# A two-layer transformer trunk on one core: the attention rounds put into traced order, in two groups of matmul steps instead of four

## The chip, the cores and the metric

One core of a Trainium2 chip runs the whole program. Its engines are TensorE (PE, with its weight loads shown as PEld), VectorE (DVE), ScalarE (ACT), GpSimd (POOL) and SyncE (SP, which issues the weight transfers). The metric is the device time of one execution in microseconds (us); a kernel is timed several times and the median is compared.

## The reference

Two decoder layers over 256 tokens of width 1024. Each layer is a half-step SwiGLU (width 2816), an attention mixer, a second half-step SwiGLU and a gated layer input. The mixer of the first layer is latent attention (called MLA below), that of the second is forgetting attention (FOX); both have 16 heads and are causal. Cut to the mixers:

```python
def mla_mixer(hn, pos, w_in, g_q_lat, w_uq, g_kv_lat, w_ukv, g_qn, g_kn, w_o):
    z = hn @ w_in                                   # c_q 512, c_kv 256, k_pe 32
    q = rms_norm(c_q, g_q_lat) @ w_uq               # 16 heads x 96
    kv = rms_norm(c_kv, g_kv_lat) @ w_ukv           # 16 heads x (64 of k, 64 of v)
    k = concatenate([k_nope, k_pe of every head])
    q, k = rms_norm per head, rope on the last 32
    return attention(q, k, v) @ w_o
def fox_mixer(hn, w_in, b_f, g_qn, g_kn, w_o):
    q, k, v, f = split(hn @ w_in)                   # 16 heads x 64 each, 16 gates
    return attention(rms_norm(q), rms_norm(k), v, cumsum(log_sigmoid(f + b_f))) @ w_o
def attention(q, k, v, decay=None):                 # blocks of 128 queries
    probs = softmax(mask(q @ k.T * scale + decay[t] - decay[s]))
    return probs @ v
```

## The kernel before, in words

**Dense products.** A weight unit of up to 1 MB is loaded by SP into one of three `raw` buffers. ScalarE rounds it to `whi` (L92) and VectorE writes the rest to `wlo` (L94), in pieces of up to 1024 columns; six pieces of each can be alive. Activations are kept as two such halves too. A dense product is then three fp32r matmuls on TensorE (`mm_w` L212 to L214, `mm_x` L225 to L227) or two in the feed-forward part (`mm_wide` L219, L220). I call these the dense matmuls.

**Attention.** The heads are worked in eight pairs per layer (class `Pair`). A pair passes four steps on TensorE: `turn` transposes its queries and keys (L543 in `heads_t`, four transposes each), and ScalarE copies the queries' transposes (`qt`, L547) and VectorE the keys' (`kt`, L545) out of PSUM; `weigh` multiplies them (L449, L450), after which VectorE masks and takes the maximum (L454), ScalarE takes the exponentials (L465), VectorE divides (L470); `turn_back` transposes the weights (L478) and a copy per head goes to `pt` (L481 on ScalarE, L483 on VectorE); `mix` multiplies them with the values (L490, L495; the two heads go to columns 0 to 63 and 64 to 127 of the array), and the result is split into two halves again (L499 on ScalarE, L294 on VectorE). All these steps take their PSUM tiles from one pool `pb` of four buffers.

**Rounds.** `mixed` weaves the pairs with the dense matmuls that are still to do: first the two last head groups of keys and queries (`late`, run by `Rows.run(amount)`, where an amount of 1 is about 1 us of dense work), then the output projection (`OutProj`). A round takes `weigh` of one pair, `turn_back` of the pair before it, `turn` of the next pair, `mix` of the second pair before, with a quarter of the dense amount behind each. Before the rounds MLA computes its latents: `zmm(c, ...)` is the product of column group c, and `latent(c)` reads it out of PSUM in a chain of ScalarE and VectorE steps that ends in a square `zq` (L696, L697, L701). `keys(g)` and `queries(g)` are the head groups' products.

**What sets the order.** The program is traced in the order of the Python code, and a scheduler then orders each engine's instructions. An instruction that went through `steady(...)` or `order(...)` while that object is on is pinned behind the instruction traced before it on its engine. In the kernel before, `steady` is off in both mixers, so that the scheduler places the attention steps and the dense matmuls as its own estimate of readiness says. Every engine runs its instructions in the order in which they then stand. At the end `OutProj.rest` does the last rows of the output projection in four parts `dp`; behind each part VectorE adds it to the residual `h` (L294). Parts 0 and 1 lie in one PSUM tile, and so do parts 2 and 3, so that part 1 is written after the addition of part 0 has read the tile.

Of the kernel before, what the change touches and what calls it, by code (L numbers as in the profile page):

```python
# [16 lines left out]
P = 128  # L17
S = 256
D = 1024
KD = D // P  # L20
# [109 lines left out]
def trunk(ctx: ExitStack, tc: tile.TileContext, a: dict, out: bass.AP):  # L130
    nc = tc.nc
# [17 lines left out]
    order = Order(tc)  # L149
# [57 lines left out]
    steady = Order(tc)  # L207
# [24 lines left out]
    for dp in range(4):  # L232
        c = slice(dp * 256, (dp + 1) * 256)
# [24 lines left out]
    ident = const.tile([P, P], F32, name="ident")  # L258
# [174 lines left out]
    class Pair:  # L433
# [10 lines left out]
        def weigh(self):  # L444
            pool, dk, qt, kt, rq = self.pool, self.dk, self.qt, self.kt, self.rq
            self.sm = []
            for hd in range(2):
                sp = pb()
                nc.tensor.matmul(sp[:, :P], lhsT=qt[:dk, hd, :P], rhs=kt[:dk, hd, :P], start=True, stop=True)  # L449
                nc.tensor.matmul(sp[:, P : 3 * P], lhsT=qt[:dk, hd, P:], rhs=kt[:dk, hd, :], start=True, stop=True)  # L450
# [12 lines left out]
                for tt, (c0, c1) in enumerate(((0, P), (P, 3 * P))):  # L463
                    sc = 1.0 if rq is None else rq[:, tt, hd : hd + 1]
                    nc.scalar.activation(  # L465
                        sm[:, c0:c1], sm[:, c0:c1], AF.Exp, bias=mx[:, 2 + tt : 3 + tt], scale=sc, accum_out=mx[:, 4 + tt : 5 + tt]
                    )
                nc.vector.reciprocal(mx[:, 6:8], mx[:, 4:6])
                for tt, (c0, c1) in enumerate(((0, P), (P, 3 * P))):
                    nc.vector.tensor_scalar(sm[:, c0:c1], sm[:, c0:c1], mx[:, 6 + tt : 7 + tt], None, op0=ALU.mult)  # L470
                self.sm.append(sm)

        def turn_back(self):
            self.pt = []
            for hd in range(2):
                tp = pb()
                for c in range(3):
                    nc.tensor.transpose(tp[:, c * P : (c + 1) * P], self.sm[hd][:, c * P : (c + 1) * P], ident)  # L478
                pt = self.pool.tile([P, 3 * P], F32, name="pt", tag="pt", bufs=4)
                if hd:  # L480
                    nc.scalar.copy(pt, tp[:, : 3 * P])  # L481
                else:
                    nc.vector.tensor_copy(pt, tp[:, : 3 * P])  # L483
                self.pt.append(pt)

        def mix(self):
            v, j, o = self.v, self.j, self.o
            op = pb()
            for n in range(2):
                nc.tensor.matmul(  # L490
                    op[n * 64 : n * 64 + 64, :S], lhsT=v[:, 0, 2 * j + n, :], rhs=self.pt[n][:, :S],
                    start=True, stop=False, skip_group_check=True,
                )
            for n in range(2):
                nc.tensor.matmul(  # L495
                    op[n * 64 : n * 64 + 64, P:S], lhsT=v[:, 1, 2 * j + n, :], rhs=self.pt[n][:, S:],
                    start=False, stop=True, skip_group_check=True,
                )
            nc.scalar.copy(o[:, j, 0, :], op[:, :S])  # L499
            tt_op(o[:, j, 1, :], op[:, :S], o[:, j, 0, :].bitcast(F32), ALU.subtract)  # L500
# [36 lines left out]
    def heads_t(pool, src, dk, name, scale):  # L537

        t = pool.tile([P, 2, S], F32, name=name, tag=name)
        tp = pb().rearrange("p (h t) -> p h t", h=2)  # L540
        for hd in range(2):
            for tt in range(2):
                nc.tensor.transpose(tp[:dk, hd, tt * P : (tt + 1) * P], src[:, tt, hd, :], ident)  # L543
        if scale is None:
            nc.vector.tensor_copy(t[:dk], tp[:dk])  # L545
        else:
            nc.scalar.activation(t[:dk], tp[:dk], AF.Copy, scale=scale)  # L547
        return t
# [90 lines left out]

    def mixed(early, late, each, ready, pair, o, after):  # L640

        order.on = True
        order.on = True
        Rows(*early).all()
        order.on = False
        order.on = False
        rows = Rows(*late)
        pairs = []
        for j in range(-1, KD + 2):
            if j == 5:  # L650
                rows.all()
            if 0 <= j - 1 < KD:
                pairs[j - 1].weigh()
                rows.run(each / 4)
            if j >= 2:
                pairs[j - 2].turn_back()
                rows.run(each / 4)
            if 0 <= j < KD:
                while not ready(j // 2):
                    rows.run(0.5)  # L660
                pairs.append(pair(j))
                pairs[j].turn()
                rows.run(each / 4)
            if j >= 2:
                pairs[j - 2].mix()
                if j == 5:
                    proj = OutProj(o, after)
                    rows = Rows(proj.first())
                    each = 3.6
                rows.run(each / 4)  # L670
        rows.all()
        proj.rest()


    def mla(norm, after, pool):
# [45 lines left out]
        sp = pb()  # L721
# [39 lines left out]
        got, ready = {}, set()  # L761
# [6 lines left out]
        v = pool.tile([P, 2, HEADS, VD], F32, name="v", tag="v", bufs=1)  # L768
        o = act.tile([P, KD, 2, S], F32R, name="xa", tag="xa")
# [92 lines left out]
        mixed([keys(0), queries(0), keys(1), queries(1)], [keys(2), queries(2), keys(3), queries(3)], 4, lambda g: g in ready, pair, o, after)  # L862


    def fox(norm, after, pool):
# [4 lines left out]
        got = {}  # L870
# [11 lines left out]
        v = pool.tile([P, 2, HEADS, VD], F32, name="v", tag="v", bufs=1)  # L882
# [87 lines left out]
        def more(g):  # L970
            yield from group(384)
            if g == 0:
                sums()
                decay(0)
            values(got.pop("ps"), 6 * g, 6)
# [6 lines left out]
        mixed([dense(0), more(0), dense(1)], [more(1), dense(2), dense(3)], 8, lambda g: len(got.get(g, ())) == 2, pair, o, after)  # L982


    def p_parts(i):
# [181 lines left out]
```

## Time and profile before

| | us |
|---|---|
| median of 3 runs | 1064.84 (1064.81 to 1066.46) |
| the profiled execution's own time | 1063.61 |
| its span, from first to last instruction | 1061.9 |
| PE busy | 1041.3 |
| DVE, ACT, POOL busy | 791.5, 591.9, 81.2 |

The profiled execution is 1.23 us below the median. A busy time counts an engine as busy while any of its instructions runs, so gaps between starts that are longer than usual do not all show as idle time; steps from start to start in the timeline show them. A row of the timeline merges instructions that are alike and follow each other; "x4" is their number. fp32 matmuls that are not transposes have two records each.

### The profile page before, as it was taken

Reading aid. Unit: us, or ns where it says so; the run is one execution under the profiler, and the core shown is the slowest. Engines: PE = TensorE matmul, PEld = TensorE weight load, DVE = VectorE, ACT = ScalarE, POOL = GpSimd, SP = SyncE. Lnnn points to the kernel's source line nnn. Section 1 sums busy time; section 2 is a strip of 40 time slices with the busy share of each in tenths; the row PEclk is TensorE's granted clock in tenths of the full one; section 3 lists DMA queues with packets and bytes.
Section 4 is the critical chain, followed back from the end, with each engine's and each line's share of the span. In section 5 each row is a group of like instructions: output and inputs, shape, how many; then the busy total and the mean of one; then the engine's idle time right before and its main releaser. Section 6 shows DMA issues by size and latency. Waiting matters only on the chain.

```text
span 1061.9 us, 16312 instructions
## 1 busy us (share of the span) xinstructions
PE 1041.3 (98%) x6368; PEld 918.9 (87%) x6368; DVE 791.5 (75%) x1364; ACT 591.9 (56%) x896; POOL 81.2 (8%) x107
## 2 busy tenths in 40 slices
PE   6999999999999999999999999999999999999998
PEld 4888888987898888888988888889999988888886
DVE  7979666679978877676987777558788797766665
ACT  4655544558766655554665555445566665554452
POOL 4000000133201000000110000011000100000010
PEclk9999999999999999999999999999999999999999
DMA  7755555534334755556447555654643266555541
GB/s 234 232 191 179 189 172 194 169 101 165 105 130 150 228 181 194 178 179 208 164 136 247 185 176 175 199 163 147 191 157 117 92 198 202 195 189 173 194 159 40
DMA packets 171089, 182.60 MB, mean 172 GB/s; under 512 B 6078, under 2 KB 164356, under 8 KB 171012
## 3 DMA queue, kind: packets, MB, share of 16 engines
q1 hardware_dynamic: 170164, 180.77, 52.1%
q8 instruction: 50, 0.82, 0.3%
q10 hardware_dynamic: 848, 0.79, 0.2%
q14 instruction: 27, 0.22, 0.1%
HBM read 180.50 MB, written 1.05 MB: 171 GB/s over the span
## 4 chain that ended last, share of the span: by engine, by line
PE 91%; DVE 4%; issue 1%; DMA 1%; POOL 1%; ACT 1%; ACTq 0%; DVEq 0%; POOLq 0%
PE pa L219 45%; PE pa L220 23%; PE pa L225 3%; PE pa L227 3%; PE pa L226 3%; PE pa L212 2%; PE pa L214 2%; PE pa L213 2%; DVE wlo L94 2%; PE pb L543 1%; PE pb L450 1%; PE pb L490 1%; PE pb L478 1%; DMA raw<-in_x_dram 1%; PE pb L449 1%
## 5 line engine op out<-in xcount | busy, mean ns | idle before, releaser
L94 DVE TENSOR_TENSOR wlo<-raw,whi 128x1024 fp32r<-128x1024 f32 (+3 forms) x357 | 425.4, 1204 | 203.6 <-ACT whi L92 203.0
L92 ACT CAST whi<-raw 128x1024 fp32r<-128x1024 f32 (+3 forms) x357 | 356.7, 1011 | 328.5 <-PE pa L219 192.9
L219 PE MATMUL pa<-xa,whi 128*128 128x512 f32 x1408 | 498.1, 397 | 1.7 <-DVE gt L294 0.9
L220 PE MATMUL pa<-xa,wlo 128*128 128x256 f32 x1408 | 396.6, 282 | 3.7 <-DVE wlo L94 3.7
L219 PEld LDWEIGHTS pa<-xa,whi 128*128 128x128 f32 x1408 | 265.4, 189 | 65.0 <-DVE gt L294 1.7
L220 PEld LDWEIGHTS pa<-xa,wlo 128*128 128x128 f32 x1408 | 264.6, 188 | 5.0 <-DVE wlo L94 4.9
L219 PE MATMUL pa<-hid,whi 128*128 128x512 f32 x704 | 244.2, 393 | 0.0
L220 PE MATMUL pa<-hid,wlo 128*128 128x256 f32 x704 | 195.0, 277 | 0.0
L219 PEld LDWEIGHTS pa<-hid,whi 128*128 128x128 f32 x704 | 132.0, 188 | 30.7
L220 PEld LDWEIGHTS pa<-hid,wlo 128*128 128x128 f32 x704 | 132.2, 188 | 0.0
L332 POOL TENSOR_TENSOR sq<-sq 128x512 f32<-128x512 f32 x24 | 35.6, 1481 | 833.6 <-ACT sq L330 805.0
L225 PE MATMUL pa<-whi,xa 128*128 128x256 f32 (+3 forms) x192 | 59.1, 308 | 0.0
L227 PE MATMUL pa<-whi,xa 128*128 128x256 f32 (+3 forms) x192 | 57.7, 301 | 0.0
L226 PE MATMUL pa<-wlo,xa 128*128 128x256 f32 (+3 forms) x192 | 57.4, 299 | 0.0
L212 PE MATMUL pa<-xa,whi 128*128 128x256 f32 x184 | 54.3, 295 | 0.0
L214 PE MATMUL pa<-xa,wlo 128*128 128x256 f32 x184 | 51.9, 283 | 0.0
L213 PE MATMUL pa<-xa,whi 128*128 128x256 f32 x184 | 51.9, 282 | 0.0
L321 DVE SCALAR_TENSOR_TENSOR xa<-h,gvec,xa 128x256 fp32r<-128x256 f32 x64 | 40.8, 679 | 2.6 <-ACT xa L319 2.6
L225 PEld LDWEIGHTS pa<-whi,xa 128*128 128x128 f32 x192 | 36.2, 189 | 1.4 <-issue 0.5
L319 ACT ACTIVATE xa<-h,gvec 128x256 fp32r<-128x256 f32 x64 | 29.0, 502 | 14.2 <-DVE h L294 12.4
L226 PEld LDWEIGHTS pa<-wlo,xa 128*128 128x128 f32 x192 | 36.2, 188 | 0.8
L227 PEld LDWEIGHTS pa<-whi,xa 128*128 128x128 f32 x192 | 36.0, 188 | 0.9
(262 smaller groups left out, 1184.0 us busy)
## 6 DMA issues: line engine op xcount, KB each, us to landing
raw<-in_ffn_w_in_dram SPq DMA_DIRECT2D x85, 1024.0 KB, 5.0
raw<-in_ffn_w_out_dram SPq DMA_DIRECT2D x32, 1024.0 KB, 5.2
raw<-in_ffn_w_out_dram SPq DMA_DIRECT2D x16, 768.0 KB, 4.8
raw<-in_ple_w_gate_dram SPq DMA_DIRECT2D x8, 1024.0 KB, 5.1
raw<-in_fox_w_in_dram SPq DMA_DIRECT2D x8, 1024.0 KB, 6.1
raw<-in_mla_w_o_dram SPq DMA_DIRECT2D x4, 1024.0 KB, 4.9
raw<-in_fox_w_o_dram SPq DMA_DIRECT2D x4, 1024.0 KB
raw<-in_mla_w_in_dram SPq DMA_DIRECT2D x3, 1024.0 KB, 5.9
```

The costliest lines, as they stand in the source:

```text
L92: self.order(self.nc.scalar.copy(h[:, part, :], whole))
L94: self.nc.vector.tensor_tensor(low[:, part, :], whole, h[:, part, :].bitcast(F32), op=ALU.subtract)
L212: steady(nc.tensor.matmul(ps, lhsT=hi, rhs=x[:, k, 0, :], start=start, stop=False, skip_group_check=True))
L213: steady(nc.tensor.matmul(ps, lhsT=hi, rhs=x[:, k, 1, :], start=False, stop=False, skip_group_check=True))
L214: return steady(nc.tensor.matmul(ps, lhsT=lo, rhs=x[:, k, 0, :], start=False, stop=stop, skip_group_check=True))
L219: steady(nc.tensor.matmul(ps, lhsT=hi, rhs=x[:, k], start=start, stop=False, skip_group_check=True))
L220: return steady(nc.tensor.matmul(ps[:, 1, :], lhsT=lo, rhs=x[:, k, 0, :], start=False, stop=stop, skip_group_check=True))
L225: steady(nc.tensor.matmul(ps, lhsT=x[:, k, 0, t], rhs=wt[0], start=start, stop=False, skip_group_check=True))
L226: steady(nc.tensor.matmul(ps, lhsT=x[:, k, 0, t], rhs=wt[1], start=False, stop=False, skip_group_check=True))
L227: steady(nc.tensor.matmul(ps, lhsT=x[:, k, 1, t], rhs=wt[0], start=False, stop=stop, skip_group_check=True))
L321: nc.vector.scalar_tensor_tensor(self.x[:, c, 1, :], h[:, c, :], g, self.x[:, c, 0, :].bitcast(F32), op0=ALU.mult, op1=ALU.subtract)
L332: nc.gpsimd.tensor_tensor(sq, sq, self.acc, op=ALU.add)
```

## The change

The rounds are rewritten. A round is now: `turn` of the next pair, then at once `turn_back` of the second pair before it, half of the dense amount, then `weigh` of the pair that was just turned, at once `mix` of the second pair before, and the other half. All matmuls of the attention steps go through `steady`, which is on during the whole of `mixed`, so that TensorE runs in traced order from the first head group's product to the end of the output projection. The dense amount per round is 2.8 instead of 4 in MLA and 6.4 instead of 8 in FOX, and 3.8 instead of 3.6 once the output projection has begun. The keys' transposes are copied by ScalarE instead of VectorE.

```diff
@@ heads_t @@
-                nc.tensor.transpose(tp[:dk, hd, tt * P : (tt + 1) * P], src[:, tt, hd, :], ident)
+                steady(nc.tensor.transpose(tp[:dk, hd, tt * P : (tt + 1) * P], src[:, tt, hd, :], ident))
         if scale is None:
-            nc.vector.tensor_copy(t[:dk], tp[:dk])
+            nc.scalar.copy(t[:dk], tp[:dk])
@@ mixed @@
-        order.on = True
+        steady.on = order.on = True
         Rows(*early).all()
         order.on = False
         rows = Rows(*late)
-        pairs = []
-        for j in range(-1, KD + 2):
-            if j == 5:
-                rows.all()
-            if 0 <= j - 1 < KD:
-                pairs[j - 1].weigh()
-                rows.run(each / 4)
-            if j >= 2:
-                pairs[j - 2].turn_back()
-                rows.run(each / 4)
-            if 0 <= j < KD:
+        pairs, proj = [], None
+        for j in range(KD + 2):
+            if j < KD:
                 while not ready(j // 2):
                     rows.run(0.5)
                 pairs.append(pair(j))
                 pairs[j].turn()
-                rows.run(each / 4)
+            if j >= 2:
+                pairs[j - 2].turn_back()
+            if j == 5:
+                rows.all()
+            rows.run(each / 2)
+            if j < KD:
+                pairs[j].weigh()
             if j >= 2:
                 pairs[j - 2].mix()
-                if j == 5:
-                    proj = OutProj(o, after)
-                    rows = Rows(proj.first())
-                    each = 3.6
-                rows.run(each / 4)
+            if j == 5:
+                proj = OutProj(o, after)
+                rows = Rows(proj.first())
+                each = 3.8
+            rows.run(each / 2)
         rows.all()
         proj.rest()
+        steady.on = False
@@ mla, fox @@
-        mixed([...], [...], 4, ...)
+        mixed([...], [...], 2.8, ...)
-        mixed([...], [...], 8, ...)
+        mixed([...], [...], 6.4, ...)
```

The matmuls of `weigh`, `turn_back` and `mix` are wrapped in `steady(...)` in the same way. Three places of the instruction order follow.

ScalarE in MLA, from behind the first pair's `qt` to behind the second pair's; first before, then the change:

```order
L92 CAST whi<-raw 128x768 x2
L803 ACTIVATE scr<-pa 128x512
L465 ACT_TABLE_LOAD
L465 ACTIVATE sm,mx<-sm,mx,rk 128x128
L465 ACTIVATE sm,mx<-sm,mx,rk 128x256
L465 ACTIVATE sm,mx<-sm,mx,rk 128x128
L465 ACTIVATE sm,mx<-sm,mx,rk 128x256
L547 ACTIVATE qt<-pb,qsc 96x512
L809 COPY kn<-pa 128x8x64
L811 ACTIVATE v<-pa,rs 128x256 x2
```

```order
L92 CAST whi<-raw 128x768 x2
L465 ACT_TABLE_LOAD
L465 ACTIVATE sm,mx<-sm,mx,rk 128x128
L465 ACTIVATE sm,mx<-sm,mx,rk 128x256
L465 ACTIVATE sm,mx<-sm,mx,rk 128x128
L465 ACTIVATE sm,mx<-sm,mx,rk 128x256
L806 ACTIVATE scr<-pa 128x512
L812 COPY kn<-pa 128x8x64
L814 ACTIVATE v<-pa,rs 128x256 x2
L551 ACTIVATE qt<-pb,qsc 96x512
L549 COPY kt<-pb 96x512
```

The second pair's `qt` now stands behind the third key group's three readouts (`scr`, `kn`, `v`), and its `kt` behind `qt`.

TensorE in MLA; first before, where the third and fourth pairs' steps stand among dense matmuls, then the change, at the end of round 4 and the first half of round 5, where the dense matmuls of `late` are used up:

```order
L478 MATMUL pb<-ident,sm 128x128 x3
L212 MATMUL pa<-xa,whi 128x256
L213 MATMUL pa<-xa,whi 128x256
L543 MATMUL pb<-ident,qn 96x128 x4
L214 MATMUL pa<-xa,wlo 128x256
L212 MATMUL pa<-xa,whi 128x256
L543 MATMUL pb<-ident,kn 96x128 x4
L213 MATMUL pa<-xa,whi 128x256
L490 MATMUL pb<-pt,v 64x256
L214 MATMUL pa<-xa,wlo 128x256
```

```order
L450 MATMUL pb<-kt,qt 128x256
L491 MATMUL pb<-pt,v 64x256 x2
L498 MATMUL pb<-pt,v 64x128 x2
L547 MATMUL pb<-ident,qn 96x128 x4
L547 MATMUL pb<-ident,kn 96x128 x4
L478 MATMUL pb<-ident,sm 128x128 x6
L449 MATMUL pb<-kt,qt 128x128
L450 MATMUL pb<-kt,qt 128x256
L449 MATMUL pb<-kt,qt 128x128
L450 MATMUL pb<-kt,qt 128x256
L491 MATMUL pb<-pt,v 64x256 x2
L498 MATMUL pb<-pt,v 64x128 x2
```

The two heads of a `mix` now always stand together (L491 x2, L498 x2), where before a first head stood alone (L490 once); and between the `mix` of one round and the `weigh` of the next there is no dense matmul.

VectorE at the end of the MLA mixer, around the additions to `h`; first before, then the change:

```order
L294 TENSOR_TENSOR xa<-pb,xa 128x256
L94 TENSOR_TENSOR wlo<-raw,whi 128x1024 x2
L294 TENSOR_TENSOR h<-h,pa 128x512 x2
L321 SCALAR_TENSOR_TENSOR xa<-h,gvec,xa 128x256 x2
L294 TENSOR_TENSOR h<-h,pa 128x512
```

```order
L294 TENSOR_TENSOR xa<-pb,xa 128x256
L94 TENSOR_TENSOR wlo<-raw,whi 128x1024
L294 TENSOR_TENSOR h<-h,pa 128x512
L294 TENSOR_TENSOR pt_in<-pb,pt_in 128x2x256
L321 SCALAR_TENSOR_TENSOR xa<-h,gvec,xa 128x256 x2
L294 TENSOR_TENSOR h<-h,pa 128x512 x2
```

Before, two parts' additions stood together; now the first part's stands alone behind the weight piece `wlo`, and the second part's matmuls wait for it.

## Rows read from the trace of the kernel before

**Rows 1.** Page, chain that ended last: shares of the span by engine.

```profile
PE 91%; DVE 4%; issue 1%; DMA 1%; POOL 1%; ACT 1%; ACTq 0%; DVEq 0%; POOLq 0%
```

**Rows 2.** Windows: stretch, length, busy PE PEld DVE ACT POOL, PEclk, DMA share, GB/s.

```profile
203.72:314.95 111.23, 109.08 (x765) 96.53 (x763) 91.78 (x301) 75.77 (x159) 27.20 (x29) 1.00 0.39 130
716.64:841.71 125.07, 123.90 (x977) 118.22 (x975) 100.06 (x295) 72.85 (x150) 6.19 (x18) 1.00 0.45 149
240.91:251.95 11.04, 10.26 (x61) 8.91 (x59) 11.04 (x36) 8.49 (x18) 4.65 (x5) 1.00 0.77 263
```

**Rows 3.** Timeline of PE, two of MLA's `mix` steps: start us, duration us, instruction.

```profile
255.62 0.65 PE L490 MATMUL pb<-pt,v 128*64 128x256 f32 x2
256.19 0.44 PE L227 MATMUL pa<-whi,zt 128*128 128x384 f32 x1
...
257.72 0.43 PE L490 MATMUL pb<-pt,v 128*64 128x256 f32 x1
...
258.51 0.50 PE L227 MATMUL pa<-whi,zt 128*128 128x512 f32 x1
...
294.41 0.65 PE L490 MATMUL pb<-pt,v 128*64 128x256 f32 x4
...
295.21 0.39 PE L214 MATMUL pa<-xa,wlo 128*128 128x256 f32 x1
```

**Rows 4.** Timeline of PE, MLA's latents and first head group.

```profile
218.96 0.50 PE L225 MATMUL pa<-whi,zt 128*128 128x512 f32 x1
...
221.82 0.28 PE L212 MATMUL pa<-xa,whi 128*128 128x256 f32 x1
...
227.47 0.35 PE L225 MATMUL pa<-whi,zt 128*128 128x384 f32 x1
...
231.96 0.34 PE L227 MATMUL pa<-whi,zt 128*128 128x384 f32 x1
233.42 0.61 PE L706 MATMUL pb<-mean_d,zq 128*128 128x1 f32 x4 [1.12 <-POOL zq L759]
```

**Rows 5.** Timeline of ACT, MLA's latents and the first two pairs.

```profile
220.81 0.60 ACT L701 ACTIVATE zq<-pa 128x512 f32<-128x512 f32 x1 [0.55 <-DVE zt L697]
...
245.71 1.57 ACT L92 CAST whi<-raw 128x768 fp32r<-128x768 f32 x2 [2.52 <-DMA raw<-in_mla_w_uq_dram]
247.18 0.59 ACT L803 ACTIVATE scr<-pa 128x512 f32<-128x512 f32 x1
247.79 1.28 ACT L465 ACT_TABLE_LOAD   x1
...
251.23 0.67 ACT L547 ACTIVATE qt<-pb,qsc 96x512 f32<-96x512 f32 x1
251.80 0.57 ACT L809 COPY kn<-pa 128x512 f32<-128x512 f32 x1
252.26 0.83 ACT L811 ACTIVATE v<-pa,rs 128x256 f32<-128x256 f32 x2
```

**Rows 6.** Timeline of PE, the first two pairs of MLA.

```profile
243.40 0.46 PE L449 MATMUL pb<-kt,qt 96*128 96x128 f32 x2
...
246.97 0.43 PE L225 MATMUL pa<-whi,zt 128*128 128x384 f32 x1
...
251.95 0.49 PE L449 MATMUL pb<-kt,qt 96*128 96x128 f32 x2 [0.73 <-ACT qt L547]
...
254.45 0.61 PE L543 MATMUL pb<-ident,qn 128*96 128x128 f32 x4 [0.21 <-DVE mx L454]
```

**Rows 7.** Timeline of DVE, end of the MLA mixer.

```profile
307.06 1.23 DVE L94 TENSOR_TENSOR wlo<-raw,whi 128x1024 fp32r<-128x1024 f32 x1 [1.73 <-ACT whi L92]
...
313.49 0.69 DVE L294 TENSOR_TENSOR h<-h,pa 128x512 f32<-128x512 f32 x1 [0.25 <-PE pa L214]
```

**Rows 8.** Timeline of PE, the first feed-forward matmuls of the program.

```profile
11.07 0.63 PE L219 MATMUL pa<-xa,whi 128*128 128x512 f32 x1
...
11.71 0.63 PE L219 MATMUL pa<-xa,whi 128*128 128x512 f32 x1
```

More of the change, by code (lines that the diff above doesn't have):

```diff
@@ L448, in weigh @@
                 sp = pb()
-                nc.tensor.matmul(sp[:, :P], lhsT=qt[:dk, hd, :P], rhs=kt[:dk, hd, :P], start=True, stop=True)
-                nc.tensor.matmul(sp[:, P : 3 * P], lhsT=qt[:dk, hd, P:], rhs=kt[:dk, hd, :], start=True, stop=True)
+                steady(nc.tensor.matmul(sp[:, :P], lhsT=qt[:dk, hd, :P], rhs=kt[:dk, hd, :P], start=True, stop=True))
+                steady(nc.tensor.matmul(sp[:, P : 3 * P], lhsT=qt[:dk, hd, P:], rhs=kt[:dk, hd, :], start=True, stop=True))
                 sm = pool.tile([P, 3 * P], F32, name="sm", tag="sm", bufs=4)
@@ L477, in turn_back @@
                 for c in range(3):
-                    nc.tensor.transpose(tp[:, c * P : (c + 1) * P], self.sm[hd][:, c * P : (c + 1) * P], ident)
+                    steady(nc.tensor.transpose(tp[:, c * P : (c + 1) * P], self.sm[hd][:, c * P : (c + 1) * P], ident))
                 pt = self.pool.tile([P, 3 * P], F32, name="pt", tag="pt", bufs=4)
@@ L489, in mix @@
             for n in range(2):
-                nc.tensor.matmul(
-                    op[n * 64 : n * 64 + 64, :S], lhsT=v[:, 0, 2 * j + n, :], rhs=self.pt[n][:, :S],
-                    start=True, stop=False, skip_group_check=True,
+                steady(
+                    nc.tensor.matmul(
+                        op[n * 64 : n * 64 + 64, :S], lhsT=v[:, 0, 2 * j + n, :], rhs=self.pt[n][:, :S],
+                        start=True, stop=False, skip_group_check=True,
+                    )
                 )
             for n in range(2):
-                nc.tensor.matmul(
-                    op[n * 64 : n * 64 + 64, P:S], lhsT=v[:, 1, 2 * j + n, :], rhs=self.pt[n][:, S:],
-                    start=False, stop=True, skip_group_check=True,
+                steady(
+                    nc.tensor.matmul(
+                        op[n * 64 : n * 64 + 64, P:S], lhsT=v[:, 1, 2 * j + n, :], rhs=self.pt[n][:, S:],
+                        start=False, stop=True, skip_group_check=True,
+                    )
                 )
@@ L640, in mixed @@
     def mixed(early, late, each, ready, pair, o, after):
-        order.on = True
-        order.on = True
+        steady.on = order.on = True
         Rows(*early).all()
         order.on = False
-        order.on = False
         rows = Rows(*late)
-        pairs = []
-        for j in range(-1, KD + 2):
-            if j == 5:
-                rows.all()
-            if 0 <= j - 1 < KD:
-                pairs[j - 1].weigh()
-                rows.run(each / 4)
-            if j >= 2:
-                pairs[j - 2].turn_back()
-                rows.run(each / 4)
-            if 0 <= j < KD:
+        pairs, proj = [], None
+        for j in range(KD + 2):
+            if j < KD:
                 while not ready(j // 2):
@@ L860, in pair @@
             return Pair(pool, qn[:, :, hs, :], kn[:, :, hs, :], QK, qsc[:QK, 0:1], v, rk[:, 0, :, hs], o, j)
-        mixed([keys(0), queries(0), keys(1), queries(1)], [keys(2), queries(2), keys(3), queries(3)], 4, lambda g: g in ready, pair, o, after)
+        mixed([keys(0), queries(0), keys(1), queries(1)], [keys(2), queries(2), keys(3), queries(3)], 2.8, lambda g: g in ready, pair, o, after)
     def fox(norm, after, pool):
@@ L980, in pair @@
             return Pair(pool, qa[:, :, hs, :], ka[:, :, hs, :], AUG, qsc[:AUG, 1:2], v, None, o, j)
-        mixed([dense(0), more(0), dense(1)], [more(1), dense(2), dense(3)], 8, lambda g: len(got.get(g, ())) == 2, pair, o, after)
+        mixed([dense(0), more(0), dense(1)], [more(1), dense(2), dense(3)], 6.4, lambda g: len(got.get(g, ())) == 2, pair, o, after)
     def p_parts(i):
```

## The prediction

> **What bounds the kernel now.** I read the chain of waits first. It lies on TensorE for 91% of the span [rows 1], so a change pays only by shortening TensorE's own steps or its waits. Next come the windows of the two mixers, the only stretches that the change touches [rows 2]. In MLA TensorE is busy for 109.08 of 111.23 us and in FOX for 123.90 of 125.07 us, so bare idle time is 2.15 and 1.17 us; whatever else there is to gain hides in steps from start to start that are longer than they need be. The third window shows what sets the early pairs of MLA: VectorE is busy for all 11.04 us of it while ScalarE is at 8.49. That speaks for handing the keys' copies to ScalarE. The timelines then show each place.
>
> **The change part by part.** The number of matmuls does not change, so I price steps and waits alone. A dense matmul of 256 columns takes a step of (227.47 - 221.82) / 48 = 0.118 us [rows 4]; 384 columns take 1.5 times that, 0.177.
>
> *The heads of a mix together.* Where the scheduler set one head alone, the step took 256.19 - 255.62 = 0.57 us for the first part and 258.51 - 257.72 = 0.79 for the rest, 1.36 together; where both heads stood together it took 295.21 - 294.41 = 0.80 [rows 3]. A visit to the half-width columns also costs about 0.1 us on either side: the dense matmul behind one lasts 0.39 us instead of 0.28 [rows 3, 4]. A split pair pays two borders more, so joining it saves 0.56 + 0.20 = 0.76 us. In MLA five of the eight pairs were split, in FOX none: **-3.8 us**. The Trainium skill ("TensorEngine Tiling (Array Packing)", section Overview) promises up to a factor of two for two 64-column tiles at work at once, against the 1.36 / 0.80 = 1.7 of the rows; by the factor of two the term would be -4.4.
>
> *MLA's latents.* The scheduler had put the first keys' product (12 matmuls from 218.96) ahead of `zmm(1)` (from 221.82). Pinned, `zmm(1)` comes first. It writes the PSUM tile that `latent(0)` still reads, and ScalarE ends that reading at 220.81 + 0.60 = 221.41 [rows 5]. TensorE is there at 218.96 [rows 4], so it stands for 2.5 us. One wait goes in exchange: the mean squares behind the first queries waited for POOL, with a step of 233.42 - 231.96 = 1.46 us instead of 0.18 [rows 4]. POOL's sum came 5.95 us after the end of `zmm(1)`, and now 12 + 24 matmuls of 2.9 + 4.2 us lie between, so that wait of 1.3 is covered. Net **+1.2 us**; both ends of this term are in rows, so I give it 0.8 to 1.6.
>
> *The second pair of MLA.* Before, from the first pair's `weigh` at 243.40 TensorE did that step, six dense matmuls and the next `turn` by 246.97, then dense matmuls that the scheduler had moved there until it waited 0.73 us for `qt` at 251.95 [rows 6]. In the new order only nine dense matmuls (1.6 us) stand there, so it asks for `qt` and `kt` 3.57 + 1.6 = 5.2 us after the first `weigh`. ScalarE is in strict order. Its queue, in steps from start to start: the two `whi` pieces start 245.71 - 243.40 = 2.3 us behind the first `weigh` (they waited for their transfer), then 1.47 for these, 1.28 for the table load, 251.23 - 249.07 = 2.16 for four exponentials, 0.61, 0.46 and 0.83 for the three readouts that now stand ahead, 0.57 for `qt` and, with the same shape, 0.67 for `kt` [rows 5]: 10.35 us. The wait is 10.35 - 5.2 = 5.2 us, less the 0.73 of before: **+4.4 us**. The transfer sets its start: SP issues a load when VectorE has emptied a `raw` buffer, so it can shift by about 1 us either way; 3.4 to 5.6.
>
> *Round 5 of MLA.* `late` holds 13.1 us of dense work (4 x 0.654 + 8 x 0.49 us for a group, twice, by the amounts in the code), which rounds 0 to 4 use up at 2.8 each. So from the `mix` of round 4 to that of round 5 TensorE has only attention steps. It cannot pass VectorE and ScalarE by more than the four `pb` buffers, and needs `qt` and `kt` at once. The trace has no such place of eight steps in a row. Below, the nearest is 251.95 to 256, with five steps and waits of 0.73 and 0.21 shown and about as much again in longer steps, 1.5 us in all [rows 6]. Above, a round's work on ScalarE that nothing covers: 2.16 + 0.57 + 0.67, two small copies of some 0.4 each (384 and 256 columns against the 512 of `qt`), and one `whi` piece of 1.05 ahead (4/3 of 1.57 / 2), 5.3 us, against 14 transposes at 0.61 for four, 2.1 us: 3.2 us. I take **+3.2 us**, the upper end, since the four buffers add waits of their own and both engines are nearly full here.
>
> *The additions to `h`.* Now part 1 of the last projection rows follows part 0 at once and waits for its addition. That stands behind a `whi` piece of 1.05 us, a `wlo` piece of 1.23 and itself takes 0.69 [rows 7], 3.0 us behind the last `mix` with a small copy ahead of it, say 3.3. TensorE covers 15 dense matmuls and four transposes, 1.77 and some 0.4 us. So **+1.1 us in each layer, +2.2**; nothing if the weight piece is early, 3.4 with no cover from the transposes.
>
> *The other rounds.* In 14 further rounds `weigh` asks for both copies after 1.4 to 3.2 us of dense work, where the scheduler before would put whatever was ready. Below: nothing, as ScalarE has time to spare over the mixers (75.77 of 111.23 and 72.85 of 125.07 us, [rows 2]); above: 14 times the 0.73 us of before, 10 us [rows 6]. In MLA a round is short against ScalarE's and VectorE's work and the copies come behind weight pieces, so I take 0.8 for each of its six, in FOX 0.1 for each of eight, 5.6; the small waits before (0.2 to 0.4 us at five places, one of them in [rows 6]) go, 1.6: **+4.0 us**. `kt` leaving VectorE is inside this term.
>
> The transfers keep their order on SP and follow VectorE's pieces; they are not late elsewhere. Sum: -3.8 + 1.2 + 4.4 + 3.2 + 2.2 + 4.0 = **+11.2 us**. On the profiled execution's 1063.61 us that is 1074.8; the median is 1.23 above that execution, so **1076.0 us** for the median of the new kernel.
>
> **The rivals.** *A, the waits are covered.* With VectorE relieved of 16 copies of 0.67 us in the stretch where it is full [rows 2], and the mixes joined, the copies might always be in time. Then -3.8 for the mixes, -1.3 for POOL's wait and -2.3 for the small ones are left, less the certain 2.5 at `zmm(1)`: 1064.84 - 4.9 = 1059.9 us. It decides if `kt` of the second pair ends within 5.2 us of the first `weigh`; the queue of ten ScalarE instructions speaks against it.
>
> *B, the waits are half of what I say.* The second pair's transfer could come 2 us earlier, round 5 cost its lower bound, and the other rounds nothing net: -3.8 + 1.2 + 2.4 + 1.5 + 1.5 = +2.8, 1067.6 us.
>
> *C, a standstill slows the clock.* The granted clock is 1.00, the 2.4 GHz level, in every window that I read [rows 2], also where TensorE stood for 1.12 us [rows 4]. At the program's start a pair of feed-forward matmuls took 11.71 - 11.07 = 0.64 us [rows 8] against 3 x 0.118 = 0.35 later, with TensorE mostly idle ahead of them. If standing 5.2 us at the second pair has that effect, the next 2 to 6 us of matmuls take 0.64 / 0.35 times as long: +1.5 to +4 us, 1079 us. The Trainium skill ("TensorE: Matmul & The Clock Gate", section "HAM oscillation — how this bites in real kernels") says that long waits between bursts bring the clock back to half; no row of before holds a wait as long, so none decides it.
>
> *D, the order doesn't bind.* If the pins changed nothing, the time would be 1064.8. The listed orders show that they bind.
>
> **How the numbers follow.** A measurement of this kernel can tell about 0.2% from no change, 2.1 us. My forecast (+7 to +15) has 0.60, C 0.14, B 0.13 (most of it above +2.1, so 0.10 slower and 0.03 the same), A 0.10, D 0.03. Faster 0.10, same 0.06, slower 0.84. The range has to hold 8 in 10: it goes from 1067 (B) to 1083 (C with the upper bounds of the transfer and the additions) and leaves out A, D and what is beyond.
>
> **What would show it.** Right: in the changed kernel's timeline of PE one wait of 4 to 6 us at L449 on ACT `kt` some 30 us into MLA, one of 2.5 at L212 on ACT `zq`, L491 always x4, two waits of about 1 us at L212 on DVE `h`; the MLA window is longer by 8 to 11 us and the FOX window by 1 to 3. Wrong: the wait at the second pair's L449 is under 2 us, or MLA is no longer than 113 us.

## The result and the profile after

| | before | changed |
|---|---|---|
| median (us) | 1065.01 (1064.81 to 1066.46, 4 runs) | 1084.37 (1081.40 to 1086.05, 4 runs) |
| profiled execution: own time, span (us) | 1063.61, 1061.9 | 1081.40, 1079.7 |
| ratio | | 1.0165 (95% interval 1.0146 to 1.0184) |

The kernel became slower by 19.4 us in the medians and by 17.8 us in the profiled executions. The sign is the one predicted. The size is at the far end: the median, 1084.4, lies 1.4 us above the range's upper end, 1083, while the ratio times 1064.84, the median that the prediction started from, is 1082.4, just inside; either is well above the 1076.0 that was named. (The two medians alone have a ratio of 1.0182, which lies in the interval.)

The chain that ended last now lies on TensorE for 87% of the span, against 91% [rows 1]. ScalarE's share rose from 1 to 3%, that of issue (time in which the engine waited for nothing that the profile shows) from 1 to 3 and that of the DMA from 1 to 2.

```profile
PE 87%; DVE 4%; ACT 3%; issue 3%; DMA 2%; POOL 1%; ACTq 0%; DVEq 0%; POOLq 0%
```

To compare stretches I cut both traces at the same dense matmuls: from the 1051st to the 1651st (the MLA mixer and a little of what follows) and from the 3901st to the 4801st (FOX). Windows of the kernel before, then of the changed one; columns as in [rows 2].

```profile
202.67:331.63 128.96, 126.81 (x862) 111.65 (x861) 107.27 (x323) 85.95 (x174) 34.02 (x33) 1.00 0.39 129
714.68:872.00 157.32, 156.15 (x1159) 146.09 (x1157) 126.99 (x331) 91.75 (x178) 13.00 (x22) 1.00 0.45 149
```

```profile
202.27:344.79 142.52, 129.82 (x862) 115.38 (x861) 107.06 (x315) 90.57 (x182) 30.50 (x33) 0.94 0.36 117
729.00:887.45 158.45, 155.53 (x1159) 144.36 (x1157) 124.13 (x324) 96.42 (x186) 11.32 (x22) 1.00 0.45 148
```

MLA is longer by 13.6 us, FOX by 1.1. The remaining 3.1 us lie in unchanged code: the cuts' own times give -0.4 ahead of MLA, +1.2 between the mixers and +2.3 behind FOX. In one such place 152 feed-forward matmuls took 26.50 us in the changed kernel (from 914.00) and 26.16 before (from 898.17), with TensorE busy throughout and the granted clock at 1.00 in both. The kernel without pins below, whose mixers are faster than before, has +1.4 and +1.2 us at the same cuts, so I do not count these as the change's.

So the question is MLA. This is the view of TensorE's waits in that stretch (line that waited, releaser, us in total, how often, the longest), first before, then changed:

```profile
PE pb L706 <- POOL zq L759: 1.1, 1, 1.1
PE pb L449 <- ACT qt L547: 0.7, 1, 0.7
...
```

```profile
PE pb L449 <- ACT kt L549: 6.4, 2, 5.3
PE pa L212 <- ACT zq L704: 2.4, 1, 2.4
PE pb L478 <- DVE pt L483: 1.1, 1, 1.1
PE pa L212 <- DVE h L294: 1.0, 1, 1.0
PE pa L226 <- DVE wlo L94: 0.9, 1, 0.9
PE pb L478 <- DVE xa L294: 0.4, 1, 0.4
PE pb L547 <- DVE mx L454: 0.2, 1, 0.2
PE pb L478 <- DVE mx L454: 0.2, 1, 0.2
```

2.0 us became 12.6. The second thing to see is PEclk in the windows: its mean over MLA fell from 1.00 to 0.94. Windows of the changed kernel in three places show where, behind the stand at `zmm(1)`, from the second pair's `weigh` on and from round 5's:

```profile
222.00:225.20 3.20, 3.20 (x17) 3.20 (x16) 0.93 (x7) 0.00 (x0) 0.00 (x0) 0.50 0.02 5
257.96:262.80 4.84, 4.83 (x15) 4.48 (x16) 3.40 (x14) 2.80 (x8) 0.00 (x0) 0.50 0.04 14
287.87:293.50 5.63, 5.63 (x22) 4.09 (x23) 3.35 (x22) 1.50 (x5) 0.00 (x0) 0.50 0.56 186
```

A granted clock of 0.50 is 1.2 GHz, the lower of TensorE's two levels; 1.00 is 2.4 GHz. At the second pair and in round 5 the clock is already at 0.50 in the wait ahead of `weigh`; at `zmm(1)` it falls after the first six dense matmuls.

The timeline of PE shows waits and slower steps (start us, duration us, instruction, idle ahead and releaser); it answers to [rows 3, 4, 6].

```profile
218.32 0.30 PE L727 MATMUL pb<-ident,kpet 32*128 32x32 f32 x2
221.06 0.38 PE L212 MATMUL pa<-xa,whi 128*128 128x256 f32 x1 [2.43 <-ACT zq L704]
...
222.04 0.42 PE L213 MATMUL pa<-xa,whi 128*128 128x256 f32 x1
...
225.24 0.33 PE L213 MATMUL pa<-xa,whi 128*128 128x256 f32 x1
...
247.41 0.49 PE L449 MATMUL pb<-kt,qt 96*128 96x128 f32 x2
...
252.32 0.34 PE L227 MATMUL pa<-whi,zt 128*128 128x384 f32 x1
257.96 0.80 PE L449 MATMUL pb<-kt,qt 96*128 96x128 f32 x2 [5.31 <-ACT kt L549]
...
282.13 0.65 PE L491 MATMUL pb<-pt,v 128*64 128x256 f32 x4
...
282.94 0.64 PE L547 MATMUL pb<-ident,qn 128*96 128x128 f32 x4
...
286.23 0.55 PE L478 MATMUL pb<-ident,sm 128*128 128x128 f32 x3 [1.10 <-DVE pt L483]
287.87 0.79 PE L449 MATMUL pb<-kt,qt 96*128 96x128 f32 x2 [1.10 <-ACT kt L549]
...
290.73 1.12 PE L491 MATMUL pb<-pt,v 128*64 128x256 f32 x4
...
292.20 0.58 PE L212 MATMUL pa<-xa,whi 128*128 128x256 f32 x1
...
324.08 0.39 PE L212 MATMUL pa<-xa,whi 128*128 128x256 f32 x1 [1.02 <-DVE h L294]
```

Behind the stand at `zmm(1)` 15 dense matmuls of 256 columns took 225.24 - 222.04 = 3.20 us, 0.213 each, against the 0.118 of [rows 4]. A mix took 282.94 - 282.13 = 0.81 us ahead of round 5 and 292.20 - 290.73 = 1.47 in it. At the lower level a step is 1.8 times as long.

ScalarE's timeline between the two pairs answers to [rows 5]:

```profile
250.07 1.57 ACT L92 CAST whi<-raw 128x768 fp32r<-128x768 f32 x2 [2.71 <-DMA raw<-in_mla_w_uq_dram]
251.66 1.28 ACT L465 ACT_TABLE_LOAD   x1
...
255.09 0.58 ACT L806 ACTIVATE scr<-pa 128x512 f32<-128x512 f32 x1
...
256.76 0.68 ACT L551 ACTIVATE qt<-pb,qsc 96x512 f32<-96x512 f32 x1
257.33 0.58 ACT L549 COPY kt<-pb 96x512 f32<-96x512 f32 x1
```

The first `weigh` starts at 247.41 and `kt` of the second pair ends at 257.91, 10.5 us later: the queue that the prediction added up to 10.35.

### The profile page after: what moved, and what is told of

Same layout as the page of the kernel before. It is cut to its first block, busy times and chain, and to the rows that moved or that the text cites. A ratio compares the mean times of both kernels' runs of the same rounds, so it can differ in the third digit from the quotient of the medians.

```text
span 1079.7 us, 16326 instructions
## 1 busy us (share of the span) xinstructions
PE 1047.1 (97%) x6368; PEld 923.3 (86%) x6368; DVE 788.5 (73%) x1348; ACT 601.4 (56%) x912; POOL 77.2 (7%) x107
## 4 chain that ended last, share of the span: by engine, by line
PE 87%; DVE 4%; ACT 3%; issue 3%; DMA 2%; POOL 1%; ACTq 0%; DVEq 0%; POOLq 0%
PE pa L219 43%; PE pa L220 22%; PE pa L225 2%; PE pa L226 2%; PE pa L227 2%; PE pa L212 2%; PE pa L213 2%; PE pa L214 2%; DVE wlo L94 2%; PE pb L450 1%; ACT whi L92 1%; PE pb L547 1%; PE pb L491 1%; PE pb L449 1%; PE pb L478 1%
## 5 line engine op out<-in xcount | busy, mean ns | idle before, releaser
L219 PEld LDWEIGHTS pa<-xa,whi 128*128 128x128 f32 x1408 | 265.4, 188 | 65.3 <-DVE gt L294 1.4
L220 PE MATMUL pa<-hid,wlo 128*128 128x256 f32 x704 | 197.4, 280 | 0.0
L226 PE MATMUL pa<-wlo,xa 128*128 128x256 f32 (+3 forms) x192 | 57.3, 298 | 0.0
L321 DVE SCALAR_TENSOR_TENSOR xa<-h,gvec,xa 128x256 fp32r<-128x256 f32 x64 | 43.7, 728 | 2.7 <-ACT xa L319 2.7
L212 PEld LDWEIGHTS pa<-xa,whi 128*128 128x128 f32 x184 | 35.5, 193 | 7.3 <-DVE h L294 2.9
L226 PEld LDWEIGHTS pa<-wlo,xa 128*128 128x128 f32 x192 | 36.1, 188 | 0.8
```

The lines of the kernel that those rows point to most:

```text
L212: steady(nc.tensor.matmul(ps, lhsT=hi, rhs=x[:, k, 0, :], start=start, stop=False, skip_group_check=True))
L219: steady(nc.tensor.matmul(ps, lhsT=hi, rhs=x[:, k], start=start, stop=False, skip_group_check=True))
L220: return steady(nc.tensor.matmul(ps[:, 1, :], lhsT=lo, rhs=x[:, k, 0, :], start=False, stop=stop, skip_group_check=True))
L226: steady(nc.tensor.matmul(ps, lhsT=x[:, k, 0, t], rhs=wt[1], start=False, stop=False, skip_group_check=True))
L321: nc.vector.scalar_tensor_tensor(self.x[:, c, 1, :], h[:, c, :], g, self.x[:, c, 0, :].bitcast(F32), op0=ALU.mult, op1=ALU.subtract)
```

## The experiments

My theory from these profiles: the pinned order makes TensorE stand in MLA, and behind the longer stands the clock falls to half, which the sum did not hold. Rivals: the keys' copies on ScalarE, the smaller amounts, strict order of any kind, or chance. A table of all runs ahead of the details. "MLA" is the stretch between the same two matmuls, PEclk its mean granted clock, both from the windows of each profile; ratios are to the kernel before, run beside it (its medians were 1066.3 to 1067.8 there), so that runs of different groups are compared by the ratio and not by the median.

| run | median us | ratio (95%) | MLA us | PEclk |
|---|---|---|---|---|
| before | 1065.01 | 1 | 128.96 | 1.00 |
| changed | 1084.37 | 1.0165 (1.0146 to 1.0184) | 142.52 | 0.94 |
| e5 changed again | 1083.51 | 1.0148 (1.0115 to 1.0181) | 142.58 | 0.94 |
| e4 stands filled | 1076.74 | 1.0092 (1.0061 to 1.0123) | 138.18 | 1.00 |
| e2 early groups not pinned | 1077.59 | 1.0090 (1.0060 to 1.0119) | 137.87 | 0.95 |
| e1 `kt` on VectorE | 1077.51 | 1.0100 (1.0067 to 1.0133) | 139.84 | 0.98 |
| e3 no pins | 1063.82 | 0.9963 (0.9948 to 0.9977) | 126.59 | 1.00 |
| e12 no pins, again | 1065.00 | 0.9987 (0.9973 to 1.0001) | 126.70 | 1.00 |
| e7 no pins, `kt` on VectorE | 1064.05 | 0.9969 (0.9952 to 0.9985) | 127.94 | 1.00 |
| e8 no pins, mix head by head | 1064.87 | 0.9977 (0.9958 to 0.9995) | 127.98 | 0.99 |
| e10 no pins, old amounts | 1065.99 | 1.0002 (0.9988 to 1.0016) | 127.90 | 1.00 |
| e13 no pins, amounts 2 and 5 | 1065.85 | 0.9998 (0.9984 to 1.0013) | 126.79 | 1.00 |
| e11 pins, placed by hand | 1077.44 | 1.0101 (1.0079 to 1.0124) | 138.37 | 0.98 |
| e6 before, `kt` on ScalarE | 1069.05 | 1.0014 (0.9999 to 1.0028) | 130.72 | 1.00 |

**Filling the stands (e4).** This separates the clock from the waits: useless matmuls, which write a PSUM tile that nobody reads, stand where TensorE stood.

```diff
+    def idle(x, n):
+        ip = pb()
+        for _ in range(n):
+            tc.keep_in_program_order(nc.tensor.matmul(ip[:, :S], lhsT=x[:, 0, 0, :P], rhs=x[:, 0, 0, :], ...))
@@ mla @@
+        idle(x, 20)
         zmm(1, w.get(), range(KD))
@@ mixed @@
+            if x is not None and j in (1, 5):
+                idle(x, 42 if j == 1 else 20)
             if j < KD:
                 pairs[j].weigh()
```

> The changed kernel with 82 extra matmuls of 256 columns of no use, put into the three stands of MLA (20 ahead of zmm(1), 42 ahead of the second pair's weigh, 20 ahead of round 5's). No other instruction changes its place. Theory (the clock fell because TensorE stood, and the half clock behind the stands cost 4 to 6 us on top of the waits): the granted clock stays at 1.00 through MLA, and though TensorE does 9.7 us more work the time falls by 3 to 6 us, to 1078 to 1081. Rival 1 (the clock falls for another reason, or its loss is hidden in waits that follow): same time within 1 us. Rival 2 (the extra matmuls delay what follows): slower by 1 to 3 us.

Measured: MLA 138.18 us, 4.3 less than the changed kernel though TensorE does 82 matmuls more in it, and a clock of 1.00. The window of MLA, then the timeline of PE at the three places (L648 is the filling):

```profile
202.47:340.65 138.18, 133.29 (x944) 119.77 (x943) 106.50 (x315) 90.11 (x182) 32.04 (x33) 1.00 0.38 121
```

```profile
218.52 0.31 PE L736 MATMUL pb<-ident,kpet 32*128 32x32 f32 x2
218.76 2.65 PE L648 MATMUL pb<-xa 128*128 128x256 f32 x20
221.26 0.39 PE L212 MATMUL pa<-xa,whi 128*128 128x256 f32 x1
...
251.00 5.19 PE L648 MATMUL pb<-xa 128*128 128x256 f32 x42
256.42 0.49 PE L449 MATMUL pb<-kt,qt 96*128 96x128 f32 x2 [0.23 <-ACT kt L549]
...
279.36 0.60 PE L450 MATMUL pb<-kt,qt 96*128 96x256 f32 x2
...
284.07 2.64 PE L648 MATMUL pb<-xa 128*128 128x256 f32 x20 [0.85 <-DVE pt L483]
286.55 0.39 PE L449 MATMUL pb<-kt,qt 96*128 96x128 f32 x2
```

The wanted matmuls start as late as in the changed kernel (`zmm(1)` 2.74 us behind the last transposes in both, the second pair's `weigh` 10.50 us behind the first's for 10.55), so the waits are still there, and what came back is the clock's part: 4.3 us net. In round 5 the filling overran the wait by some 0.9 us (7.19 us from L450's last start to the next L449, against 287.87 - 281.61 = 6.26), so the clock's full part is nearer to 5.2. The slow steps themselves lost more: the three windows at 0.50 hold 13.7 us of work, and at steps 1.8 times as long that is 6.1 us lost (an estimate), 2.2 of them at the second pair. Waits that came back balance a part of it: e4 has 0.45 and 0.31 us on `kt` at the third and fourth pairs, where the changed kernel has none. The time, 1076.7 us, is even below the 1078 to 1081 of the theory; both rivals fell.

**The kernel again (e5).** No edit.

> The changed kernel once more, unchanged, beside the next three and with a trace of its own. Theory (stands are made by the order, and the clock falls behind the long ones): the stands come again at the same places with the same lengths within 0.3 us, and the half clock behind zmm(1), behind the second pair's weigh and in round 5 again; 1081 to 1088. Rival (the clock's fall is chance): the stands come again, but at least one of the three stretches at half clock is missing or lies elsewhere, with a time nearer to 1078.

Measured: MLA 142.58 us. The stands were 2.43, 0.89, 5.01, 1.10, 1.09 and 1.02 us, each where it was, and half clock came at the same three places. With e4, that puts the clock's fall down to the order of the work and not to chance. In this execution the granted clock was also 0.68 from 20 to 30 us, near the program's start, and the 1051st dense matmul came at 204.37 us against 202.27.

**No pins (e3, repeated as e12).** The new rounds, the new amounts and `kt` on ScalarE stay; only the pins go.

```diff
-        steady.on = order.on = True
+        order.on = True
         Rows(*early).all()
```

> The changed kernel without any pin on the matmuls of the mixers; the new rounds, their amounts and the copy of kt on ScalarE stay. Theory (strict order makes the waits): the scheduler fills the second pair's wait with dense matmuls again, so no stand over 1.5 us is left in MLA and the granted clock stays at 1.00 there; MLA comes back to 112 to 115 us, the whole to 1064 to 1069. Rival (the new rounds with smaller amounts are too short for ScalarE and VectorE, whatever the order): the waits stay in another place, 1076 or more.

> The kernel without pins once more (amounts 2.8 and 6.4), in more rounds. Theory (the scheduler's places plus joined mixes beat both kernels): ratio to before 0.995 to 0.998, with no stand over 1.5 us in MLA and the clock at 1.00 there. Rival (its lead was this chip's or this execution's luck): ratio 0.999 to 1.001.

Measured: 1063.82 and 1065.00 us; MLA is shorter than before's by 2.4 and 2.3 us, where the theory of e3 had it 1 to 4 us longer, and the longest stand in it is 1.45 and 1.55 us. The repeat missed its own theory, with a ratio of 0.9987 for 0.998 at most and a stand just over 1.5. TensorE's waits in MLA in e3:

```profile
PE pa L225 <- ACT v L814: 1.4, 1, 1.4
PE pb L709 <- POOL zq L762: 1.1, 1, 1.1
```

Without the pins 26 dense matmuls stand between the second pair's `turn` and its `weigh`, instead of nine, dense work of the output projection stands in rounds 4 and 5, and all 16 pairs' mixes are joined. The whole loss in MLA, 142.52 - 126.59 = 15.9 us, therefore hangs on the pins. The lead over before has an interval clear of 1 in the first run and one that touches 1 in the second. Both profiles show MLA shorter by the same amount, so I take the lead in MLA as shown, and its size in the whole, 0.1 to 0.4%, as only roughly known. No version with a higher lead was found; e7 below can't be told from it.

**Early groups not pinned (e2).**

```diff
-        steady.on = order.on = True
+        order.on = True
         Rows(*early).all()
         order.on = False
+        steady.on = True
```

> The changed kernel, but the matmuls are pinned only after the early head groups (the pin is switched on one step later, in both mixers). Theory: the first keys' product stands ahead of zmm(1) again, so the stand of 2.4 us at 218.3 goes, and with it the 3.4 us at half clock behind it (some 1.5 us of loss); the wait for POOL's sum of 1.1 us comes back: 3 us less than the changed kernel, 1080 to 1082; the second pair and round 5 stay as they are. Rival (the first stand costs only itself, the clock falls there anyway): 1.3 us less, 1083.

Measured: 1077.6 us, under the 1080 to 1082 expected, and MLA 137.87 us, 4.7 less than the changed kernel for the 3 expected. The stand at `zmm(1)` and the half clock behind it are gone. The wait on POOL's sum is back at 1.1, and two more things went that I had not counted: the 0.9 us at L226 on `wlo`, and 0.7 of the second pair's stand (4.63 for 5.31). The stands of the second pair and of round 5, and half clock behind each, stayed.

**Where the keys are copied (e1, e7, e6).** In e1 and e7 one line of the change is undone, with and without pins; e6 is the kernel before with that line alone.

```diff
-            nc.scalar.copy(t[:dk], tp[:dk])
+            nc.vector.tensor_copy(t[:dk], tp[:dk])
```

> The changed kernel with one line back: the keys' transposes are copied by VectorE. Theory (the time went to the pinned order: three long stands in MLA and what the clock loses behind them; the copies' engine is a side matter): the second pair's stand before L449 stays at 4 us or more, since qt still stands behind ScalarE's queue, and loses only kt's 0.6 us; other copies of kt now stand behind VectorE's longer queue. Time within 2 us of the changed kernel, 1082 to 1086. Rival (handing kt to ScalarE is what costs): at least half of the 19 us comes back, 1075 or less.

> The kernel without pins (new rounds and amounts), with the keys' copies back on VectorE. Theory (the gain over before is the joined mixes, 3.1 us of steps in MLA): one pair's mix is split instead of none, so it stays within 1.5 us of the kernel without pins and is 2 to 4 us faster than before. Rival (the copies on ScalarE made the gain): no faster than before.

> The kernel before with one line of the change: ScalarE copies the keys' transposes. Theory (the kernel without pins won its 4 us by mixes whose heads stand together, not by the copies): seven pairs' mixes are split here against five, so nothing is won; within 2 us of before or up to 3 slower. Rival (VectorE's relief is what the kernel without pins gained): 3 to 4 us faster than before.

Measured: with pins (e1) 1077.5 us, between the two expectations. MLA is 2.7 us shorter, but its waits are not fewer; the first pair now waits as well (1.7 us on `msq`), and the second pair's stand is 3.0 us on `qt` instead of 5.3 on `kt`:

```profile
PE pb L449 <- ACT qt L551: 3.9, 3, 3.0
...
PE pb L449 <- DVE msq L851: 1.7, 1, 1.7
...
```

The eight groups of that view come to 13.6 us against the changed kernel's 12.6, while PEclk rose from 0.94 to 0.98. What came back is clock, since round 5's half clock was missing and the second pair's was shorter. Without pins (e7) the line changes MLA by 1.35 us (127.94 for 126.59) and the time by nothing that can be told; on the kernel before (e6) it wins nothing, with seven pairs split instead of five. So the keys' copies are not the source of the gain of e3. With pins they are no side matter, as I had it: the one line brings the ratio from 1.0165 and 1.0148 to 1.0100, in MLA through the clock.

**How a mix is traced (e8).** e3 with the second loop of `mix` folded into the first, so that one head's 256 and 128 columns come ahead of the other head's.

```diff
             for n in range(2):
                 steady(nc.tensor.matmul(op[... , :S], ...))
-            for n in range(2):
                 steady(nc.tensor.matmul(op[... , P:S], ...))
```

> The kernel without pins, but mix traces all matmuls of its first head ahead of those of the second, so that the two halves of the array's columns never stand next to each other with like shapes: 256 and 128 columns of one head, then of the other. Theory (two heads side by side run at once: 0.80 us a pair against 1.36 where they are apart): 0.56 x 16 = 9 us more than the kernel without pins, 7 to 10. Rival (what a split mix costs is the dense matmul between its heads): 1 us more or less.

Measured: 1064.87 us, a ratio of 0.9977 for e3's 0.9963, far from 9 us more. The timeline of PE:

```profile
270.54 0.66 PE L491 MATMUL pb<-pt,v 128*64 128x256 f32 x4
271.02 0.40 PE L497 MATMUL pb<-pt,v 128*64 128x128 f32 x4
271.35 0.64 PE L546 MATMUL pb<-ident,qn 128*96 128x128 f32 x4
```

The mix takes 271.35 - 270.54 = 0.81 us as before, and both heads' 256 columns are recorded ahead of both heads' 128, though the program has them head by head. That is the order of the changed kernel's pinned mixes, so as far as the records go the edit did not change what ran, and the run tests neither the theory nor the rival. My theory's condition is refuted by the trace of before, where unlike shapes of the two halves run at once: the second head's 256 columns start at 257.72 [rows 3] and the first head's 128 beside them:

```profile
257.73 0.43 PE L495 MATMUL pb<-pt,v 128*64 128x128 f32 x2
```

In that split mix the first head's 256 columns had run alone at 255.62, with a full-width dense matmul behind them. That this matmul is what a split costs fits these rows, but no run isolates it. The 1.4 us that e8's MLA lost against e3 lie at the second pair, where the stand is 2.02 us instead of 1.45 and is followed by half clock (granted clock 0.79 from 252 to 260 us, where e3 has 1.00).

**The amounts (e10, e13).** e3 with 4 and 8 per round, and with 2 and 5, instead of 2.8 and 6.4.

> The kernel without pins, with the amounts of before in the rounds (4 in MLA, 8 in FOX; 3.8 for the projection stays). Theory (without pins the amounts move little, since the scheduler fills by readiness; the gain is the joined mixes, of which one is split here): within 1.5 us of the kernel without pins, 2 to 4 us faster than before. Rival (the smaller amounts made the gain): as before, within 1 us.

> The kernel without pins with still smaller amounts, 2 in MLA and 5 in FOX. Theory (what counts without pins is whether mixes are joined and stands stay short, and both are as in the kernel with 2.8 and 6.4): within 1.5 us of it. Rival (the smaller the amount the better, as 4 and 8 against 2.8 and 6.4 had it by 2 us): 1.5 to 3 us faster than it.

Measured: ratios 1.0002 and 0.9998. e10 missed its expectation of 2 to 4 us under before. In its profile MLA is 1.3 us longer than e3's and FOX 157.66 against 156.85. In e13 MLA is as short as in e3, but FOX takes 158.63. The amounts move the time by 1 to 2 us at most, and the intervals of e12 and e13, which ran together, overlap; neither a trend nor a best amount is shown.

**Pins with the places chosen by hand (e11).** Behind the early groups MLA is pinned again; `plan` gives the dense amount of each half round, and the output projection begins in round 3.

```diff
+        order.on = True
         Rows(*early).all()
         order.on = False
+        steady.on = plan is not None
+        begin = 5 if plan is None else 3
...
-            rows.run(each / 2)
+            rows.run(plan[2 * j])
@@ mla @@
-        mixed([...], [...], 2.8, ...)
+        mixed([...], [...], 2.8, ..., [2.1, 1.4, 4.6, 0, 2.4, 0, 0, 0, 2.6, 0, 1.2, 1.4, 2.4, 0.4, 2.4, 0.4, 2.0, 0.8, 2.0, 0.8])
```

> Matmuls pinned in MLA from behind the early head groups to the end of the output projection, as in the changed kernel, but with the dense amounts put by hand where the kernel without pins has them: 4.6 us of dense work between turn and weigh of the second pair instead of 1.4, and the output projection begun in round 3 with the rows of the first pairs, so that rounds 4 and 5 have dense work. FOX without pins. Theory (not the pin costs, but the places that it freezes: no dense work where ScalarE is late): no stand over 1.5 us behind the early groups but the 1.1 at the addition to h, clock 1.00 through MLA, MLA 1 us either side of the kernel without pins; 1062 to 1067 where before has 1067. Rival (strict order itself costs, since each small lateness of ScalarE or VectorE is paid at once): MLA 5 us or more longer than without pins, 1069 or more.

Measured: 1077.4 us and MLA 138.37; the rival's numbers came true. The second pair's stand did go down to 1.3 us (a dense matmul that waits for `v`, as in e3), but others came in the rounds behind it:

```profile
PE pa L212 <- ACT xa L503: 2.2, 1, 2.2
PE pb L478 <- ACT qt L551: 1.6, 2, 1.2
PE pa L225 <- ACT v L817: 1.3, 1, 1.3
PE pa L213 <- DVE xa L294: 1.3, 2, 0.8
...
```

The first and the fourth are my plan's own fault, which asks for a mix's result right behind that mix. The others are small latenesses that a strict order pays at once. The clock fell twice, to 0.50 from 269.3 and from 286.4 us, each time behind waits of 0.5 to 1.2 us with nothing but transposes between them. It did not fall behind the longest stand, the first of the list, which lies between a mix and dense matmuls (291.97 to 294.22 us):

```profile
290.00:296.00 6.00, 3.28 (x23) 2.31 (x22) 3.28 (x17) 2.49 (x9) 0.00 (x0) 1.00 0.00 0
```

So a stand's length alone does not tell whether half clock follows. Whether a better table of places would do as well as no pins is not settled by this.

## Why the prediction was right or wrong

**Right: the waits.** The prediction's terms for MLA come to -3.8 + 1.2 + 4.4 + 3.2 + 1.1 + 4.8 - 1.6 = +9.3 us. With the clock held at full speed (e4) MLA is 138.18 - 128.96 = 9.2 us longer with round 5's overrun of 0.9, 8.3 without it. That the sum agrees so closely is partly luck, since some terms were off against each other:

- *The second pair's stand*: 5.2 us predicted, 5.31 measured, on ACT `kt` as named, with ScalarE's queue at 10.5 us for 10.35. Right.
- *The stand at `zmm(1)`*: 2.5 predicted, 2.43 measured, on ACT `zq`; POOL's wait vanished as said. The net of 1.2 was too small all the same: e2 shows that the place is worth 4.7 us, through the clock, a new wait of 0.9 at L226 and 0.7 more at the second pair.
- *Round 5*: 3.2 predicted. From 282.94 to 287.87 TensorE did 14 transposes in 4.93 us, for which the prediction allowed 2.1: 2.8 lost ahead of `weigh`, where half clock sets in. Right, a little high.
- *The additions to `h`*: 1.1 each predicted, 1.02 in each layer. Right.
- *The other rounds*: too dear in MLA, where the only waits outside the places above are 0.9 us at L226 on `wlo` and 0.4 at L478, against 4.8 put on them. In FOX new waits of 0.5 us on `kt` and 0.2 on `qt`, both at one place, are near the 0.8 put on its rounds; FOX is longer by no more than 1.1 us in all, since TensorE's busy time in it fell by 0.6.
- *Joined mixes*: 0.81 us a pair at full clock (282.13 to 282.94), none split, as predicted. The -3.8 was not measured by itself. In e3, at a clock of 1.00, TensorE's busy time in MLA is 126.81 - 123.66 = 3.2 us less than before, which holds every other change of place too; so the term was a little too large at best.
- *The signs named*: the second pair's stand lies 50 us into MLA and not some 30 (before, its `weigh` stood 251.95 - 203.72 = 48 us in [rows 2, 6], so that was misread). MLA grew by 13.6 us, beyond the 8 to 11 named, and FOX by 1.1 of 1 to 3.

**Wrong: rival C's reach.** The step that failed is "If standing 5.2 us at the second pair has that effect, the next 2 to 6 us of matmuls take 0.64 / 0.35 times as long: +1.5 to +4 us", with a chance of 0.14 and outside the sum. For that one place it was good: steps 1.8 times as long for 4.8 us, some 2.2 us lost. But the clock fell three times: behind the stand of 2.43 us too, and in round 5, where only transposes stand among waits of 0.2, 0.2 and 1.1 us ahead of the fall. Together it cost 4.3 us net, which the sum held at nothing. The rows of before could not have told: the longest wait that I took from them was 1.12 us, and they said nothing of 2.5. Yet the sum itself held a stand of 2.5, and I never asked the question of it. The rule of the Trainium skill that the prediction set beside this rival ("TensorE: Matmul & The Clock Gate", section "HAM oscillation — how this bites in real kernels") is that long waits between bursts bring the clock back to half. The trace agrees with it at the second pair (0.50 behind a wait of 5.31 us, 1.00 once e4 had filled it); round 5 fell without a wait above 1.1 us, which that rule does not cover.

**Not the change's.** Of the 17.8 us between the profiled executions, 13.6 are MLA (9.2 waits and mixes, 4.3 clock), 1.1 FOX, and 3.1 the longer steps in unchanged code. Against the 11.2 of the sum that is 4.3 of clock and 3.1 of the execution more, and 0.8 less in FOX. The median of the changed kernel lies another 3 us above its profiled execution (1084.37 and 1081.40); its other executions have mean granted clocks of 0.987 to 0.991 against 0.992 of the profiled one, and where they lost more was not recorded.

## What to carry to other kernels

A pinned order turns every lateness of another engine into a stand of the bottleneck engine, so add up the other engine's strict queue ahead of each result and put at least that much independent work between, or leave the filling to a scheduler that goes by readiness. Price each stand of TensorE twice, as the wait and, as a possible second cost, as the matmuls behind it at half clock, and ask that question at every stand of the sum, and at every stretch of transposes among short waits, not at the longest stand alone. To tell the two prices apart on the chip, fill the stands with useless matmuls: what comes back is the clock's share.

## What I had not expected

- The clock fell behind a single stand of 2.43 us (2.02 in e8), and in round 5 behind waits of at most 1.1 us each with only transposes between them. It did not fall behind stands of 1.45 us (e3) or 1.12 (before) with dense matmuls on either side, nor behind the 2.25 of e11.
- Matmuls of unlike shapes that use different 64-column halves of the array run at once (before, 257.72 and 257.73 us). Why e8's mixes ran in the same order as the changed kernel's, the records do not tell: the scheduler, a later step of the build or the chip may have regrouped them.
- With the granted clock at 1.00 and TensorE busy throughout, the same 152 matmuls took 26.16 us in one execution and 26.50 in another.
